# Transposing queries in float32 before the split, and a re-ordered opening, in an encoder kernel

## The chip, the cores and the metric

The kernel runs on one core of one Trainium2 chip. The metric is the device time of one execution in microseconds (us); the time before is the median of three runs. The engines are TensorE (PE, with its weight loads as PEld), VectorE (DVE), ScalarE (ACT), GpSimd (POOL) and SyncE (SP), which here only issues DMAs.

## The reference

Two layers of an encoder on x (256 tokens by 1024), float32. Each layer is a half-step feed-forward block, a mixing block with two attention branches, and a second half-step feed-forward block. Cut to what matters:

```
x = x + 0.5 * swiglu(rms_norm(x, ffn1_norm), ffn1_w_gate, ffn1_w_up, ffn1_w_down)
h = rms_norm(x, mix_norm);  z = h @ w_in
qa, ka, va, qs, ks, vs, zg = split(z)
qa, ka = rms_norm of each head (8 heads of 64);  qs (8 heads), ks (2 heads) likewise
o_na = neighbourhood_attention(qa, ka, va, na_rpb)      # 4 x 64 grid
o_sw = sliding_window_gqa(qs, ks, vs, t5_bias, sink)    # +-128 tokens
y = sigmoid(g_A) * (o_na @ w_branch_na) + sigmoid(g_B) * (o_sw @ w_branch_sw)
x = x + y @ w_out
x = x + 0.5 * swiglu(rms_norm(x, ffn2_norm), ...)       # 1024 -> 2816 -> 1024
```

## The kernel before

**Products in two parts.** Every float32 weight is loaded as `raw` (two rows of 128 by 512 at a time, ring of 4), then split into two fp32r tiles: `wh` is a copy made by ACT (L181), `wl` is the rest, made by DVE (L182); both lie in rings of 6. Activations are split the same way. A product is three 512-column matmuls (L167 to L169): hi by hi, hi by lo, lo by hi.

**Order.** PE's instructions run in the order in which the code emits them. What is not projected right away is put on a list by `defer` and emitted some ticks later, a tick being three matmuls of 512 columns; transpositions and attention fronts are laid between the matmuls of other projections in this way. A scheduler places the instructions of the other engines.

**Opening.** Layer 0's first feed-forward block begins with `opening`: the norm of x, the four weight pieces of column block c=0, then the squares for the row norms (ACT L214, DVE L218 and L219, POOL L173), and `second`, the four pieces of column block c=1. The gate of a column block is `sg` (ACT L448) and `hh` (DVE L449), once for each half t of the tokens. `hh` empties one of the two PSUM banks named `g`, and the projection after next writes that bank. `constants` loads the gains `qkg`, the mask and the sinks, and scales the gains on DVE (L106).

**Feed-forward.** Eleven column blocks c of 256 hidden units. The products of some of them with w_d use sums and differences of blocks; for three of these, `prepare` loads and forms the differences u and v of w_d's blocks (DVE L346) and splits them (uh, ul, vh, vl) while w_gu is still being projected: c=3 prepares 1, c=5 prepares 3, c=7 prepares 6.

**Queries.** In `mix`, a projection of 512 columns (8 heads of 64) for one half t of the tokens is normed per head (`normed`: z, sq, hv, rs_y, qn), split into `qs` with the hi and lo part of a head side by side, and 16 ticks later (18 for Q1) `turn` transposes it: one transposition for each head, 128 columns of fp32r, with hi in the first 64 partitions of the result and lo in the other 64. Two ACT copies (L499) reverse the query order and write `sqT` or `qT`. There are four such calls in a layer: Q0, Q1 (window attention) and q0, q1 (grid attention). The keys `kn` (`keys`: K0, K1, k0, k1) are transposed in float32 and split on the way out of PSUM by ACT L516 and DVE L517 into `skT` or `kT`. The first scores `sc` (L553) need Q0, Q1, K0 and K1. `qn` lies in a ring of two shared with `sq` and other tiles (tag xg), `qs` and `kn` in another ring of two (tag qk).

Of the kernel before, what the change touches and what calls it, by code (L numbers as in the profile page):

```python
# [11 lines left out]
F32 = mybir.dt.float32  # L12
F32R = mybir.dt.float32r
# [8 lines left out]
P = 128  # L22
# [28 lines left out]
HEAD = 128  # L51
PLAN = "SFGFGGFGGSS"
PREP = {3: 1, 5: 3, 7: 6}
NS = sum(kind != "S" for kind in PLAN)


@with_exitstack
def hybrid_encoder(ctx, tc, x, w_gu1, w_d1, w_in, b_gate, qk_gain, rpb, sink, t5,
# [27 lines left out]

    ident = const.tile([P, P], F32, name="ident")
    make_identity(nc, ident)
    ident_r = const.tile([P, P], F32R, name="ident_r")
    nc.vector.tensor_copy(ident_r, ident)  # L90
    mhalf = const.tile([P, 8], F32, name="mhalf")
    nc.vector.memset(mhalf, -0.5)
    warm = const.tile([P, 1], F32, name="warm")
# [6 lines left out]
    def constants():  # L100
        with tc.issue_after(rstd_done[0].ins):
            nc.gpsimd.dma_start(qkg, qk_gain)
            nc.gpsimd.dma_start(mask, c_mask)
            nc.gpsimd.dma_start(snk, bass.AP(tensor=sink.tensor, offset=sink.offset, ap=[[0, P], [1, L * NH]]))
        for g in (0, 2):
            nc.vector.scalar_tensor_tensor(qkg[:, :, g + 1], qkg[:, :, g + 1], 1.0 / math.sqrt(DH), qkg[:, :, g],  # L106
                                           op0=ALU.mult, op1=ALU.mult)
        nc.vector.tensor_scalar(nsnk, snk, -1.0, None, op0=ALU.mult)
# [113 lines left out]
    def opening(w, l):  # L222
        def piece(i, c=0):
            return load(w[l, 2 * i * P:(2 * i + 2) * P, c * 512:(c + 1) * 512].rearrange("(k p) n -> p k n", p=P),
                        2, 512)

        ps = [ps_g.tile([P, 512], F32, name="g", tag="g") for _ in range(T)]

        def steps(t, i):
            wh, wl = pieces[i]  # L230
            xh, xl = xT[t]
            for a, b in ((xh, wh), (xl, wh), (xh, wl)):
                for k in (2 * i, 2 * i + 1):
                    nc.tensor.matmul(ps[t], a[:, k, :], b[:, k % 2, :], start=a is xh and b is wh and k == 0,  # L234
                                     stop=b is wl and k == KD - 1)
            tick(2)

        pieces = []
        chain["act"] = warmed
        warmup(5)  # L240
        norm(0, 0, 0, True)
        pieces.append(piece(0))
        warmup(5)
        fetch(1, 0)
        norm(1, 0, 0, True)
        pieces.append(piece(1))
        fetch(0, 1)
        fetch(1, 1)
        warmup(3)
        steps(0, 0)  # L250
        norm(0, 0, 1, True)
        steps(1, 0)
        pieces.append(piece(2))
        norm(1, 0, 1, True)
        pieces.append(piece(3))
        square(0, 0, idle)
        square(0, 1, idle)
        second = [piece(0, 1)]
        square(1, 0, idle)
        square(1, 1, idle)  # L260
        second += [piece(i, 1) for i in range(1, KD // 2)]
        chain.clear()
        for i in (1, 2, 3):
            for t in range(T):
                steps(t, i)
        defer(24, "constants", constants)
        return ps, second

    def project(t, pieces, n):
# [34 lines left out]
    def ffn(l, n, w_gu, w_d, after):  # L304
        with tc.tile_pool(name="ffn", bufs=1) as fp:
# [128 lines left out]
            for c in range(NFC):  # L434
# [4 lines left out]
                    pieces = second  # L439
                else:  # L440
                    pieces = columns(w_gu, l, c * 512, 512)
                if c in PREP:
                    prepare(PREP[c])
                pair = act.tile([P, T, FC], F32, name="hh", tag="xg", bufs=2)
                for t in range(T):
                    ps = both[t] if first else project(t, pieces, 512)
# [25 lines left out]
    def mix(l, n, after):  # L472
        with tc.tile_pool(name="mix", bufs=1) as mp:
# [11 lines left out]
                                        r.unsqueeze(2).to_broadcast([P, nh, DH]), ALU.mult)  # L485

            def queries(key, ps, t, qT):
                qn = act.tile([P, NH, DH], F32, name="qn", tag="xg", bufs=2)
                normed(ps, t, NH, qn)
                qs = mp.tile([P, NH, 2, DH], F32R, name="qs", tag="qk", bufs=2)  # L490
                split_to(qs[:, :, 0, :], qs[:, :, 1, :], qn)

                def turn():
                    for half in range(2):
                        tp = ps_tp.tile([P, 4, P], F32R, name="tp", tag="tp")
                        for j in range(4):
                            nc.tensor.transpose(tp[:, j, :], qs[:, 4 * half + j].rearrange("p two d -> p (two d)"),
                                                ident_r)
                        nc.scalar.activation(qT[:, 4 * half:4 * half + 4, t * P:(t + 1) * P], flipped(tp), AF.Copy)  # L499

                defer(QK_LAG + MORE.get(key, 0), key, turn)

# [23 lines left out]
            def attend(name, ins, qT, kh, kl, kidx, bias_of, vcol, ready, oT, sink_l=None):  # L526
# [12 lines left out]
                def front(h):  # L539
# [10 lines left out]
                    sm = small.tile([P, T], F32, name="sm", tag="sm")  # L550
                    for t in range(T):
                        for i, k in enumerate((kh, kl)):
                            nc.tensor.matmul(ps[:, t, :], qT[:, h, t * P:(t + 1) * P], k[:, kidx(h), :],  # L553
                                             start=i == 0, stop=i == 1)
                    for t in range(T):
                        nc.vector.tensor_tensor_reduce(S_[:, t, :], ps[:, t, :], b(t), -1.0, least,  # L556
# [44 lines left out]
                both = mp.tile([P, 2, *shape], F32R, name=name, tag=tag)  # L601
                return both[:, 0], both[:, 1]

            sqT = mp.tile([P, NH, S], F32R, name="sqT", tag="sq")
            skT = pair("skT", "sk", [2, S])
            sv = mp.tile([P, T, 2, 3 * DH], F32R, name="sv")
            qT = mp.tile([P, NH, S], F32R, name="qT")
            kT = (mp.tile([P, NH, S], F32R, name="kh", tag="kh"), mp.tile([P, NH, S], F32R, name="kl"))
            va = mp.tile([P, T, NH, P], F32R, name="va")
            oB = pair("oB", "oB", [4, T, P])  # L610
# [219 lines left out]
```

## Time and profile before

| | before |
|---|---|
| median of 3 runs (1077.96 to 1079.82) | 1078.34 us |
| profiled execution, own time | 1079.11 us |
| its span, first to last instruction | 1077.3 us |
| PE busy | 1069.9 us, 99% |
| DVE busy | 876.0 us, 81% |
| ACT busy | 671.9 us, 62% |
| POOL busy | 116.5 us, 11% |
| granted TensorE clock, mean | 0.999 |

The own time lies 1.8 us over the span; that much passes around the instructions. PE is busy nearly all the time; the other engines are read here by where PE waits for them.

### The profile page before, as it was taken

What the parts mean: (1) busy time and instruction counts of PE and PEld (TensorE: products, weight loads), DVE (VectorE), ACT (ScalarE), POOL (GpSimd) and SP (SyncE); (2) the same over time, 40 slices, a digit from 0 to 9 for tenths busy, and PEclk for the clock granted to TensorE, in tenths of its full rate; (3) what the DMA queues carried; (4) which work ended last, traced back from release to release, by engine and by line L of the source; (5) the groups of instructions that cost most, each with busy time, mean ns of one, the idle gap of its engine ahead of it and who ended that gap; (6) DMA issues with size and microseconds to landing.
All of it is one profiled execution on the core that took longest, in us unless ns stands there. A gap on an engine that the chain in (4) does not pass through costs nothing.

```text
span 1077.3 us, 14747 instructions
## 1 busy us (share of the span) xinstructions
PE 1069.9 (99%) x5125; PEld 890.8 (83%) x5125; DVE 876.0 (81%) x1337; ACT 671.9 (62%) x1014; POOL 116.5 (11%) x118
## 2 busy tenths in 40 slices
PE   9999999999999999999999999999999999999998
PEld 7888888888888888888878888888888888888887
DVE  6788798889886768879877787988898866778796
ACT  6565654788764556565465665657887646566562
POOL 1000030243420000000000000003534100000000
PEclk9999999999999999999999999999999999999999
DMA  7777565765654567756647765548566554776652
GB/s 241 233 248 236 181 201 181 215 195 159 192 193 136 192 202 244 240 175 201 202 158 233 227 212 201 192 149 241 181 196 179 184 172 161 232 231 207 200 194 78
DMA packets 98827, 212.63 MB, mean 197 GB/s; under 512 B 7568, under 2 KB 13744, under 8 KB 98752
## 3 DMA queue, kind: packets, MB, share of 16 engines
q1 hardware_dynamic: 98560, 211.60, 62.2%
q8 instruction: 40, 0.66, 0.2%
q14 instruction: 35, 0.29, 0.1%
q0 software_dynamic: 192, 0.08, 0.1%
HBM read 210.59 MB, written 1.06 MB: 196 GB/s over the span
## 4 chain that ended last, share of the span: by engine, by line
PE 96%; DVE 2%; DMA 1%; issue 1%; ACT 0%; ACTq 0%; DVEq 0%
PE g L167 21%; PE g L169 21%; PE g L168 21%; PE acc L167 5%; PE acc L169 5%; PE acc L168 5%; PE tp L314 2%; PE sc L553 1%; PE po L588 1%; PE tp L169 1%; PE tp L167 1%; PE tp L168 1%; PE pt L574 1%; DMA raw<-in_w_gu 1%; PE tp L198 1%; PE g L234 1%
## 5 line engine op out<-in xcount | busy, mean ns | idle before, releaser
L182 DVE TENSOR_TENSOR wl<-raw,wh 128x1024 fp32r<-128x1024 f32 x336 | 404.9, 1217 | 71.8 <-ACT wh L181 69.7
L181 ACT ACTIVATE wh<-raw 128x1024 fp32r<-128x1024 f32 x336 | 346.5, 1044 | 132.4 <-DMA raw<-in_w_gu 50.2
L167 PE MATMUL g<-wh,xh 128*128 128x512 f32 (+1 forms) x976 | 383.9, 393 | 0.5 <-DVE hh L449 0.5
L168 PE MATMUL g<-wl,xh 128*128 128x512 f32 (+1 forms) x976 | 377.6, 387 | 1.1 <-DVE wl L182 1.1
L169 PE MATMUL g<-wh,xl 128*128 128x512 f32 (+1 forms) x976 | 377.9, 387 | 0.7 <-DVE xl L182 0.7
L169 PEld LDWEIGHTS g<-wh,xl 128*128 128x128 f32 x976 | 183.3, 188 | 40.0 <-DVE xl L182 2.1
L168 PEld LDWEIGHTS g<-wl,xh 128*128 128x128 f32 x976 | 183.7, 188 | 34.6 <-DVE wl L182 1.9
L167 PEld LDWEIGHTS g<-wh,xh 128*128 128x128 f32 x976 | 183.6, 188 | 33.8 <-DVE hh L449 1.1
L448 ACT ACTIVATE sg<-g,rs_y 128x256 f32<-128x256 f32 x88 | 41.1, 467 | 85.8 <-PE g L169 73.6
L449 DVE SCALAR_TENSOR_TENSOR hh<-g,rs_y,sg 128x256 f32<-128x256 f32 x88 | 42.2, 479 | 49.6 <-ACT sg L448 49.5
L167 PE MATMUL acc<-wh,hi 128*128 128x512 f32 x180 | 71.1, 395 | 0.0
L169 PE MATMUL acc<-wh,lo 128*128 128x512 f32 x180 | 70.2, 390 | 0.0
L168 PE MATMUL acc<-wl,hi 128*128 128x512 f32 x180 | 70.1, 389 | 0.0
L173 POOL TENSOR_TENSOR rs_y<-ms,mhalf 128x1 f32<-128x1 f32 x12 | 6.7, 557 | 554.8 <-DVE ms L219 546.4
L346 DVE TENSOR_TENSOR u<-raw 128x512 f32<-128x512 f32 x64 | 41.9, 685 | 18.2 <-DMA raw<-in_w_d 18.1
L181 ACT ACTIVATE corner<-raw 128x512 fp32r<-128x512 f32 x32 | 20.2, 631 | 50.6 <-DMA raw<-in_w_d 28.3
L566 POOL TENSOR_TENSOR S<-S,sm 128x512 f32<-128x512 f32 x32 | 37.2, 1161 | 65.6 <-DVE sm L565 42.4
L169 PEld LDWEIGHTS acc<-wh,lo 128*128 128x128 f32 x180 | 33.8, 188 | 7.2
L168 PEld LDWEIGHTS acc<-wl,hi 128*128 128x128 f32 x180 | 33.8, 188 | 6.8
L167 PEld LDWEIGHTS acc<-wh,hi 128*128 128x128 f32 x180 | 33.8, 188 | 6.7
L559 ACT ACTIVATE S<-S,mx 128x256 f32<-128x256 f32 x64 | 31.9, 499 | 8.0 <-DVE mx L556 7.9
L182 DVE TENSOR_TENSOR lo<-a,hi 128x896 fp32r<-128x896 f32 x32 | 33.7, 1083 | 0.0
(189 smaller groups left out, 1511.7 us busy)
## 6 DMA issues: line engine op xcount, KB each, us to landing
raw<-in_w_gu SPq DMA_DIRECT2D x176, 512.0 KB, 4.4
raw<-in_w_d SPq DMA_DIRECT2D x100, 512.0 KB, 4.1
raw<-in_w_in SPq DMA_DIRECT2D x64, 512.0 KB, 4.5
raw<-in_w_out SPq DMA_DIRECT2D x16, 512.0 KB, 3.6
bb<-in_b_gate SPq DMA_DIRECT2D x16, 256.0 KB, 3.7
raw<-in_w_bsw SPq DMA_DIRECT2D x8, 512.0 KB, 3.8
raw<-in_w_bna SPq DMA_DIRECT2D x8, 512.0 KB, 3.6
raw<-in_w_d SPq DMA_DIRECT2D x12, 256.0 KB, 2.5
```

What stands on the lines that cost most here:

```text
L167: nc.tensor.matmul(ps, xh, wh, start=first, stop=False)
L168: nc.tensor.matmul(ps, xh, wl, start=False, stop=False)
L169: nc.tensor.matmul(ps, xl, wh, start=False, stop=last)
L181: linked("act", lambda: nc.scalar.activation(hi, src, AF.Copy))
L182: linked("dve", lambda: nc.vector.tensor_tensor(lo, src, hi.bitcast(F32), ALU.subtract))
L198: nc.tensor.transpose(tp[:, i, :], xs[t][:, k * P:(k + 1) * P], ident)
L314: nc.tensor.transpose(tp[:, SLOT[t][i], :], hh[:, t, i * P:(i + 1) * P], ident)
L346: sub = lambda to, x, y: nc.vector.tensor_tensor(to, x, y, ALU.subtract)
L448: nc.scalar.activation(sg, ps[:, :FC], AF.Silu, scale=rstd[t])
L449: nc.vector.scalar_tensor_tensor(pair[:, t], ps[:, FC:], rstd[t], sg, op0=ALU.mult, op1=ALU.mult)
L559: nc.scalar.activation(S_[:, t, :], S_[:, t, :], AF.Exp, bias=mx[:, t:t + 1], scale=-1.0, accum_out=sm[:, t:t + 1])
L566: nc.gpsimd.tensor_tensor(S_, S_, sm.unsqueeze(2).to_broadcast([P, T, S]), ALU.mult)
```

## The change

Four things change. (1) `queries` no longer splits before it transposes. `qn` takes the place of `qs` in the ring qk, four float32 transpositions turn two heads each, and the split is done from PSUM: for even and for odd heads one ACT copy and one DVE subtraction of 64 partitions by 4 heads by 128. In `sqT` and `qT` the even heads now stand ahead of the odd ones, and the score matmul indexes them so; hi and lo of a head still fill 128 partitions. `ident_r` and its cast are gone. (2) In the opening, two pieces of c=1 instead of one stand ahead of the squares of x1. (3) The scaling of `qkg` and `snk` is emitted at tick 70 and no longer with their loads. (4) In the first feed-forward block alone, the three `prepare` calls stand at c=5, 7 and 8.

```
-PREP = {3: 1, 5: 3, 7: 6}
+PREP = {3: 1, 5: 3, 7: 6}
+PREP_FIRST = {5: 1, 7: 3, 8: 6}
...
-    ident_r = const.tile([P, P], F32R, name="ident_r")
-    nc.vector.tensor_copy(ident_r, ident)
...
+    def scaled():
         for g in (0, 2):
             nc.vector.scalar_tensor_tensor(qkg[:, :, g + 1], ...)
...
-        second = [piece(0, 1)]
+        second = [piece(i, 1) for i in range(2)]
         square(1, 0, idle)
         square(1, 1, idle)
-        second += [piece(i, 1) for i in range(1, KD // 2)]
+        second += [piece(i, 1) for i in range(2, KD // 2)]
...
         defer(24, "constants", constants)
+        defer(70, "scaled", scaled)
...
-                if c in PREP:
-                    prepare(PREP[c])
+                prep = PREP if n else PREP_FIRST
+                if c in prep:
+                    prepare(prep[c])
...
             def queries(key, ps, t, qT):
-                qn = act.tile([P, NH, DH], F32, name="qn", tag="xg", bufs=2)
+                qn = mp.tile([P, 2, NH, DH], F32, name="qn", tag="qk", bufs=2)[:, 0]
                 normed(ps, t, NH, qn)
-                qs = mp.tile([P, NH, 2, DH], F32R, name="qs", tag="qk", bufs=2)
-                split_to(qs[:, :, 0, :], qs[:, :, 1, :], qn)
 
                 def turn():
-                    for half in range(2):
-                        tp = ps_tp.tile([P, 4, P], F32R, name="tp", tag="tp")
-                        for j in range(4):
-                            nc.tensor.transpose(tp[:, j, :], qs[:, 4 * half + j].rearrange("p two d -> p (two d)"),
-                                                ident_r)
-                        nc.scalar.activation(qT[:, 4 * half:4 * half + 4, t * P:(t + 1) * P], flipped(tp), AF.Copy)
+                    tp = ps_tp.tile([P, 4, P], F32, name="tp", tag="tp")
+                    for j in range(4):
+                        nc.tensor.transpose(tp[:, j, :], qn[:, 2 * j:2 * j + 2].rearrange("p two d -> p (two d)"), ident)
+                    cols = slice(t * P, (t + 1) * P)
+                    for e in range(2):
+                        a, b = e * DH, (1 - e) * DH
+                        split_to(qT[a:a + DH, e, :, cols], qT[b:b + DH, e, :, cols], flipped(tp[a:a + DH]))
...
-                            nc.tensor.matmul(ps[:, t, :], qT[:, h, t * P:(t + 1) * P], k[:, kidx(h), :],
+                            nc.tensor.matmul(ps[:, t, :], qT[:, h % 2, h // 2, t * P:(t + 1) * P], k[:, kidx(h), :],
```

The changed file is one to three lines longer, so L181 and L182 become L182 and L183, L448 and L449 become L451 and L452, and so on.

DVE in the opening, before: `wl_219`, `wl_232`, `wl_238` and `wl_244` are the four pieces of c=1, `hh_283` the gate of c=0 (`g_107` the bank of its first half).

```order
L182 TENSOR_TENSOR wl_219<-raw_216,wh_218 128x1024
L449 SCALAR_TENSOR_TENSOR hh_283<-g_107,rs_y_214,sg_284 128x256
L218 TENSOR_TENSOR ms_224<-ssq_140 128x1
L219 TENSOR_SCALAR ms_224<-ms_224 128x1
L182 TENSOR_TENSOR wl_232<-raw_229,wh_231 128x1024
L182 TENSOR_TENSOR wl_238<-raw_235,wh_237 128x1024
L106 SCALAR_TENSOR_TENSOR qkg_94<-qkg_94 128x2 x2
L182 TENSOR_TENSOR wl_244<-raw_241,wh_243 128x1024
L449 SCALAR_TENSOR_TENSOR hh_283<-g_108,rs_y_227,sg_287 128x256
```

The same place on DVE with the change; the four pieces are `wl_217`, `wl_223`, `wl_236` and `wl_242`.

```order
L183 TENSOR_TENSOR wl_217<-raw_214,wh_216 128x1024
L183 TENSOR_TENSOR wl_223<-raw_220,wh_222 128x1024
L452 SCALAR_TENSOR_TENSOR hh_281<-g_105,rs_y_212,sg_282 128x256
L219 TENSOR_TENSOR ms_228<-ssq_138 128x1
L220 TENSOR_SCALAR ms_228<-ms_228 128x1
L183 TENSOR_TENSOR wl_236<-raw_233,wh_235 128x1024
L183 TENSOR_TENSOR wl_242<-raw_239,wh_241 128x1024
L452 SCALAR_TENSOR_TENSOR hh_281<-g_106,rs_y_231,sg_285 128x256
L107 SCALAR_TENSOR_TENSOR qkg_92<-qkg_92 128x2 x2
```

The second piece now stands ahead of the first gate, and the scaling of the gains stands behind the second gate instead of between two pieces. On ACT the copy of the second piece moves in the same way, ahead of the first square of x1, with `sg` of the first half behind that square as before.

DVE in the window between the transposition of Q1 and the first scores of layer 0, before: `skT` are the two halves of the window attention's keys, `kn_2042` the normed K1, `qn_2106` and `qs_2117` belong to q1.

```order
L481 TENSOR_REDUCE hv_2111<-sq_2109 128x8
L484 TENSOR_TENSOR kn_2042<-z_2043,rs_y_2050 128x2x64
L482 TENSOR_SCALAR hv_2111<-hv_2111 128x8
L182 TENSOR_TENSOR wl_2200<-raw_2197,wh_2199 128x1024
L182 TENSOR_TENSOR wl_2206<-raw_2203,wh_2205 128x1024
L484 TENSOR_TENSOR qn_2106<-z_2107,rs_y_2114 128x512
L517 SCALAR_TENSOR_TENSOR skT_1813<-tp_2145,qkg_94,skT_1813 128x2x128
L182 TENSOR_TENSOR wl_2357<-raw_2354,wh_2356 128x1024
L182 TENSOR_TENSOR wl_2363<-raw_2360,wh_2362 128x1024
L517 SCALAR_TENSOR_TENSOR skT_1813<-tp_2162,qkg_94,skT_1813 128x2x128
L182 TENSOR_TENSOR qs_2117<-qn_2106,qs_2117 128x8x64
```

The same place with the change; `tp_2113` is Q1's transposed block, and the two rows that read it write the low parts of its even and odd heads.

```order
L487 TENSOR_TENSOR kn_2031<-z_2032,rs_y_2039 128x2x64
L484 TENSOR_REDUCE hv_2100<-sq_2098 128x8
L485 TENSOR_SCALAR hv_2100<-hv_2100 128x8
L183 TENSOR_TENSOR wl_2180<-raw_2177,wh_2179 128x1024
L183 TENSOR_TENSOR sqT_1810<-tp_2113,sqT_1810 64x4x128
L183 TENSOR_TENSOR wl_2186<-raw_2183,wh_2185 128x1024
L519 SCALAR_TENSOR_TENSOR skT_1811<-tp_2128,qkg_92,skT_1811 128x2x128
L487 TENSOR_TENSOR qn_2095<-z_2096,rs_y_2103 128x512
L183 TENSOR_TENSOR wl_2331<-raw_2328,wh_2330 128x1024
L183 TENSOR_TENSOR sqT_1810<-tp_2113,sqT_1810 64x4x128
L183 TENSOR_TENSOR wl_2337<-raw_2334,wh_2336 128x1024
L519 SCALAR_TENSOR_TENSOR skT_1811<-tp_2145,qkg_92,skT_1811 128x2x128
```

Two subtractions now stand between `kn` and the second `skT`; the split of q1 that followed the second `skT` is gone from there.

DVE in column block c=3 of the first feed-forward block, before: the pieces of w_gu are the rows `wl`, and `u_486`, `ul1_490` belong to `prepare`.

```order
L346 TENSOR_TENSOR u_486<-raw_484,raw_482 128x512
L346 TENSOR_TENSOR u_486<-raw_482 128x512
L182 TENSOR_TENSOR lo4_408<-tp_397,hi4_407 128x512
L327 TENSOR_TENSOR a_413<-a_413 128x128 x3
L182 TENSOR_TENSOR wl_473<-raw_470,wh_472 128x1024
L327 TENSOR_TENSOR a_413<-a_413 128x128
L182 TENSOR_TENSOR ul1_490<-u_486,uh1_489 128x1024
L182 TENSOR_TENSOR wl_479<-raw_476,wh_478 128x1024
L182 TENSOR_TENSOR lo7_412<-a_413,hi7_411 128x896
L182 TENSOR_TENSOR wl_560<-raw_557,wh_559 128x1024
L449 SCALAR_TENSOR_TENSOR hh_371<-g_430,rs_y_227,sg_455 128x256
```

The same place with the change, where the rows of `prepare` are missing.

```order
L183 TENSOR_TENSOR lo4_406<-tp_395,hi4_405 128x512
L329 TENSOR_TENSOR a_411<-a_411 128x128 x4
L183 TENSOR_TENSOR wl_468<-raw_465,wh_467 128x1024
L183 TENSOR_TENSOR lo7_410<-a_411,hi7_409 128x896
L183 TENSOR_TENSOR wl_474<-raw_471,wh_473 128x1024
L183 TENSOR_TENSOR wl_537<-raw_534,wh_536 128x1024
L452 SCALAR_TENSOR_TENSOR hh_369<-g_425,rs_y_231,sg_450 128x256
```

The three u and ul rows ahead of the last `hh` are gone, and with them their loads of w_d on SP's queue; PE's order is as before but for the eight blocks of transpositions.

## Rows read from the trace of the kernel before

**Rows 1.** The page: span, PE's busy line, the chain by engine.

```profile
span 1077.3 us, 14747 instructions
...
PE 1069.9 (99%) x5125; PEld 890.8 (83%) x5125; DVE 876.0 (81%) x1337; ACT 671.9 (62%) x1014; POOL 116.5 (11%) x118
...
PE 96%; DVE 2%; DMA 1%; issue 1%; ACT 0%; ACTq 0%; DVEq 0%
```

**Rows 2.** The waits of PE: total us, times, longest.

```profile
PE g L168 <- DVE wl L182: 1.1, 2, 0.7
...
PE g L167 <- DVE hh L449: 0.5, 1, 0.5
```

**Rows 3.** The timeline of PE in the opening: start, us, engine, line.

```profile
20.28 0.45 PE L167 MATMUL g<-wh,xh 128*128 128x512 f32 x1
20.57 0.40 PE L168 MATMUL g<-wl,xh 128*128 128x512 f32 x1
20.80 0.40 PE L169 MATMUL g<-wh,xl 128*128 128x512 f32 x1
...
27.48 0.40 PE L167 MATMUL g<-wh,xh 128*128 128x512 f32 x1
```

**Rows 4.** The timeline of ACT in the opening.

```profile
17.33 1.04 ACT L181 ACTIVATE wh<-raw 128x1024 fp32r<-128x1024 f32 x1
18.28 0.58 ACT L214 ACTIVATE idle<-x 128x512 f32<-128x512 f32 x1
...
19.18 0.47 ACT L448 ACTIVATE sg<-g,rs_y 128x256 f32<-128x256 f32 x1 [0.20 <-PE g L234]
```

**Rows 5.** The timeline of DVE in the opening.

```profile
18.41 1.23 DVE L182 TENSOR_TENSOR wl<-raw,wh 128x1024 fp32r<-128x1024 f32 x1 [0.60 <-ACT wh L181]
19.69 0.48 DVE L449 SCALAR_TENSOR_TENSOR hh<-g,rs_y,sg 128x256 f32<-128x256 f32 x1
```

**Rows 6.** The timeline of PE at the end of column block c=3.

```profile
49.91 0.39 PE L169 MATMUL g<-wh,xl 128*128 128x512 f32 x1
50.78 0.50 PE L167 MATMUL g<-wh,xh 128*128 128x512 f32 x1 [0.48 <-DVE hh L449]
51.12 0.39 PE L168 MATMUL g<-wl,xh 128*128 128x512 f32 x1
```

**Rows 7.** The timeline of DVE in column block c=3.

```profile
42.09 1.29 DVE L346 TENSOR_TENSOR u<-raw 128x512 f32<-128x512 f32 x2 [2.53 <-DMA raw<-in_w_d]
```

**Rows 8.** The timeline of PE: a float32 block of the norm, then Q1's block.

```profile
185.67 0.60 PE L198 MATMUL tp<-ident,x 128*128 128x128 f32 x4
186.03 0.48 PE L167 MATMUL acc<-wh,hi 128*128 128x512 f32 x1
...
217.28 0.80 PE L497 MATMUL tp<-ident_r,qs 128*128 128x128 f32 x8
217.92 0.46 PE L167 MATMUL g<-wh,xh 128*128 128x512 f32 x1
```

**Rows 9.** Groups of DVE by line and shape: busy us, mean ns.

```profile
L182 DVE TENSOR_TENSOR pl<-pt,ph 128x512 fp32r<-128x512 f32 x32 | 21.8, 680 | 2.8 <-ACT ph L181 2.7
...
L182 DVE TENSOR_TENSOR qs<-qn,qs 128x512 fp32r<-128x512 f32 x8 | 5.5, 682 | 0.0
```

**Rows 10.** The timeline of DVE between Q1's block and the first scores.

```profile
217.50 0.69 DVE L481 TENSOR_REDUCE hv<-sq 128x8 f32<-128x512 f32 x1 [1.02 <-ACT sq L479]
218.19 0.29 DVE L484 TENSOR_TENSOR kn<-z,rs_y 128x128 f32<-128x128 f32 x1
...
225.38 0.48 DVE L517 SCALAR_TENSOR_TENSOR skT<-tp,qkg,skT 128x256 fp32r<-128x256 f32 x1
```

**Rows 11.** The timeline of PE at the first scores.

```profile
226.03 0.64 PE L553 MATMUL sc<-skT,sqT 128*128 128x256 f32 x4
```

**Rows 12.** Windows of the first feed-forward block: busy us and instructions of each engine.

```profile
95.40:107.10 11.70, 11.70 (x53) 9.63 (x52) 9.91 (x11) 6.98 (x8) 0.00 (x0) 1.00 0.90 290
107.10:118.90 11.80, 11.80 (x58) 9.85 (x57) 9.30 (x16) 7.47 (x10) 0.00 (x0) 1.00 0.58 187
```

More of the change, by code (lines that the diff above doesn't have):

```diff
@@ L602, in pair @@
                 return both[:, 0], both[:, 1]
-            sqT = mp.tile([P, NH, S], F32R, name="sqT", tag="sq")
+            sqT = mp.tile([P, 2, NH // 2, S], F32R, name="sqT", tag="sq")
             skT = pair("skT", "sk", [2, S])
             sv = mp.tile([P, T, 2, 3 * DH], F32R, name="sv")
-            qT = mp.tile([P, NH, S], F32R, name="qT")
+            qT = mp.tile([P, 2, NH // 2, S], F32R, name="qT")
             kT = (mp.tile([P, NH, S], F32R, name="kh", tag="kh"), mp.tile([P, NH, S], F32R, name="kl"))
```

## The prediction

> **What bounds the kernel now.** I read the page first: PE is busy 1069.9 of 1077.3 us and holds 96% of the chain that ended last [rows 1]. Time therefore goes only by PE's own instructions, or by the few moments in which PE waits. The view of PE's waits is short: two waits on `wl` (1.1 us together) and one on `hh` (0.5 us) concern this change [rows 2]; the two on `wl` stand in column block c=1, the one on `hh` at the end of c=3. Then I read PE's starts in the timelines, because they price a wait or a block of transpositions better than the modelled durations do: a 512-column matmul follows the one before after 0.23 us (20.57 to 20.80) [rows 3]. DVE is the engine that PE waits for, so its order decides what the edits beside it cost.
>
> **Queries: what PE saves.** A block of eight fp32r transpositions holds the next matmul back by 217.92 - 217.28 = 0.64 us; a block of four float32 transpositions holds it back by 186.03 - 185.67 = 0.36 us [rows 8]. The new block is of the second kind, float32, 128 by 128, four of them, so PE saves 0.28 us a call, 0.56 for the two calls of a branch, and 2.24 us for eight calls, if nothing takes it back. Two heads side by side are to PE one more float32 tile of 128 by 128, as those of `x` are; I see no row from which the new ones could cost more.
>
> The Trainium skill, "FP8 and Floating Point Precision", section "TensorE Precision Notes", says that true FP32 takes four passes through the PE array, which speaks against this edit. By that rule, with a quarter of eight fp32r transpositions' 0.64 us (0.08 us) as one pass, four float32 ones would take 4 x 4 x 0.08 = 1.28 us instead of 0.36, and each call would lose 0.64 us. The rows of four float32 transpositions show 0.36 us, so the rule as it stands doesn't hold for these blocks, and the measurement decides.
>
> **Queries: what the other engines do.** Before, a call costs DVE one subtraction from SBUF (`qs`, 0.682 us); now it costs two of 64 partitions by 512 elements from PSUM. The nearest row is `pl` from `pt`, 0.680 us for 512 elements in each of 128 partitions [rows 9]. I take 0.68 each, since the elements in a partition are as many; an end below would be half of that, if partitions counted. DVE is thus 0.68 us a call longer; ACT has one copy less. More important is where they stand: before, the split came long before the transposition, now it lies behind it.
>
> The first scores of the window attention start at 226.03 on PE [rows 11], and the last DVE instruction that they need is the second `skT`, 225.38 + 0.48 = 225.86 [rows 10]. There is 0.17 us of slack. PE would like to be there 0.56 us sooner, at 225.47. I replay DVE from `kn` of K1. It waits for a buffer of the ring qk which Q1's block gives back, so it starts no sooner than the end of that block, about 0.5 us sooner than the 218.19 of before, say 217.65. With the change these follow back to back by the order shown: kn 0.21, hv 0.61, its scaling 0.17, wl 1.15, sqT 0.6, wl 1.15, skT 0.45, qn 0.6, wl 1.15, sqT 0.6, wl 1.15, skT 0.48 (from start to start, for which I take 0.08 us off each duration; wl by the 1.23 of [rows 5]). The sum is 8.3 us, end at about 226.0. Subtractions of 64 partitions that are cheaper by up to 0.25 us each would bring the end to 225.5. So the first scores would start between 225.6 and 226.2, and of the 0.56 us of Q0 and Q1 between 0.4 and -0.2 us is kept; I take 0.1. PE waits there in exchange for what it saved.
>
> For q0 and q1 nothing waits so closely: the pieces between them and the grid attention are many, so their 0.56 us are kept; the lower end is 0, if DVE, which is full through the fronts of the window attention, makes a later transposition wait. A layer gives 0.1 + 0.56 = 0.66, both layers 1.32 us; the ends are -0.4 and 2.24.
>
> **Opening.** Before, c=1 starts at 20.28 as soon as the first `hh` has left the bank (19.69 + 0.48 = 20.17) [rows 3, 5], and its second half starts at 27.48: 7.20 us for 24 matmuls. Without waits these take 0.29 + 23 x 0.231 = 5.60 us, so the two waits on `wl` and the slow restarts behind them cost 1.60 us. With the change ACT makes the copy of the second piece from 18.28 for 0.95 us, then the square of x1 (0.70 with the read of its sum), then `sg` at 19.93 instead of 19.18, for 0.47 us [rows 4]. DVE does the first `wl` from 18.41, the second from 19.55 to 20.77, then `hh` to 21.16. c=1 therefore starts at 21.27, 0.99 us later: a new wait, on `hh`. By then the second piece lies ready, the third follows at 23.2 (needed at 24.3) and the fourth at 24.4 (needed at 25.7), so no wait is left in it (after `sg` ACT makes the second square of x1 to 21.1 and the copies to 22.05 and 23.0, DVE's subtractions follow them; the pieces' first `wl` matmuls are the 14th and the 20th), and the second half starts at 21.27 + 5.60 = 26.87. The opening gains 0.61 us. At worst it gains nothing (the third piece late by as much); at best, if `sg` is placed as soon as before, 1.3. Scaling `qkg` behind the second gate costs nothing: DVE waits there for the gains' load, now with no urgent piece behind it, and the first reader is the keys' turn some 200 us on. The 0.16 us cast of `ident_r` lay before PE had work.
>
> **Prepare at c=5, 7 and 8.** At c=3 PE goes from 49.91 to 50.78 for one matmul, and 0.34 to the next, in place of 2 x 0.23: 0.75 us [rows 6]. It waits for an `hh` that stands on DVE behind two `u` (1.29 us [rows 7]) and one `ul` (1.2, as any `wl`). With these 2.5 us gone `hh` is no longer last, and the 0.75 us are gained. What is late next is nothing that I found.
>
> The other side is c=8. A prepare is 2 x 1.29 for u and v and 2 x 1.2 for the splits, 5.0 us of DVE, with two loads of w_d on SP's queue ahead of those of c=9. DVE is idle for 1.79 + 2.50 = 4.29 us in the two windows in which it would fall [rows 12]. The 0.7 us that do not fit shift into the window behind, where DVE has more room. I cost it at nothing; the bounds are 0 and the whole 5.0 us, if the instructions of `prepare` stand in front of a piece that PE is waiting for.
>
> **Sum.** 0.61 + 0.75 + 1.32 = 2.68 us. Against the profiled execution's own time, 1079.11, this gives 1076.43. That execution lies 0.77 us over the median of the runs shown, 1078.34, and the runs differ by up to 1.86 us; the result is a median too, so I forecast 1078.34 - 2.68 = 1075.7 us.
>
> **The rivals.** (a) All of it is kept: the subtractions of 64 partitions are short, or the scheduler's order leaves `skT` ahead of need. The gain is 0.61 + 0.75 + 2.24 = 3.6, 1074.7 us. For it speaks that DVE stands idle in the seconds before K1; against it the 0.17 us of slack at the scores.
> (b) The mix gives nothing: DVE's two extra subtractions delay `skT` and then the chain of the window attention's fronts in both layers as much as PE saved. The gain is 1.36, 1077.0 us. For it speaks that DVE is the engine waited for; against it that q0 and q1 are transposed where PE's next need is far.
> (c) The opening gives nothing, since the later `hh` starts a chain of late pieces: 2.07 us of gain, 1076.3.
> (d) On the other side: `prepare` at c=8 stands on PE's path whole. From the point at which its u and v stand ahead of the pieces of c=9 or of the last gates, each us of it is one of PE's; slower than before needs 2.68 us of the 5.0, and all of it gives 1078.34 - 2.68 + 5.0 = 1080.7 us. For it speaks that 5.0 are more than the 4.29 idle; against it that the window behind has room.
> (e) The float32 transpositions cost four passes (the rule of the page above): each call loses 0.64, 5.1 us in all, and with the opening's and c=3's gains it is 1078.34 - 1.36 + 5.1 = 1082.1 us. The rows of float32 blocks speak against it.
>
> **How the numbers follow.** The forecast has 0.50, (a) 0.17, (b) 0.20, (c) 0.05, (d) 0.07, (e) 0.01. The range goes from (a) to (b), which with (c) leave out 0.08, each widened by half of the runs' spread, 0.93 us: 1073.8 to 1077.9 us. What 0.2% is here, 2.16 us, is about what a measurement of this kernel can tell from no change; it stands at 1076.2, half a us above the forecast. Faster by more: four fifths of the forecast, nearly all of (a), a little of (b) and (c), 0.60. Slower by more: (d) and (e), with half of (d) only partly paid, 0.05. The rest, 0.35, is within 0.2%.
>
> **What the profile after would show.** Right: the new blocks hold PE for 0.36 us; PE's waits on `wl` in c=1 are gone and one on `hh` stands at about 21.3; c=1's second half starts near 26.9; no wait near 50; a short wait of the first scores on `skT` in each layer (0.3 to 0.5 us); DVE busy up by 8 x 0.68 = 5.4 us. Wrong: waits on `wl` or `hh` between 95 and 141; waits of the window attention's transpositions on DVE or ACT; a block of queries that holds PE for longer than 0.36 us; or a time above 1077.9 us, which would mean that a load or a late piece in the moved `prepare` has reached PE.

## The result, and the profile after

The changed kernel takes 1081.53 us (median of 12 runs, 1080.92 to 1083.49) against 1078.59 us for the kernel before (12 runs): a ratio of 1.0028, with a 95% interval of 1.0020 to 1.0036. It is slower by 2.9 us, where 2.7 us of gain were forecast. The profiled execution has a span of 1079.8 us and 1081.58 us of its own.

The page says at once where to look, in the busy line and the chain by engine, which answer to [rows 1].

```profile
span 1079.8 us, 14671 instructions
...
PE 1069.2 (99%) x5093; PEld 887.8 (82%) x5093; DVE 883.1 (82%) x1344; ACT 667.7 (62%) x1006; POOL 120.8 (11%) x118
...
PE 89%; DVE 6%; issue 2%; ACT 2%; DMA 1%; POOL 0%; POOLq 0%; DVEq 0%; ACTq 0%
```

PE has less to do, and still the span is longer. In the chain PE's share fell from 96 to 89%, and DVE's rose from 2 to 6%. DVE is busy for 7.1 us more: the subtractions add the 5.4 us expected, and the rest lies in other instructions, some of which took longer and some shorter than before. The view of PE's waits, in total us, times and longest, answers to [rows 2]:

```profile
PE tp L516 <- DVE qT L183: 1.2, 2, 0.6
PE pt L576 <- POOL S L568: 1.1, 2, 0.7
PE tp L516 <- DVE skT L519: 1.0, 2, 0.5
PE g L168 <- DVE hh L452: 0.8, 1, 0.8
PE g L170 <- DVE xl L183: 0.7, 1, 0.7
PE sc L555 <- DVE skT L519: 0.3, 2, 0.2
PE tp L168 <- DVE lo L183: 0.2, 1, 0.2
```

The waits on `wl` and the one at the end of c=3 are gone. In their place stand four in the mix block, each twice, once a layer: the second half of the key block k0 waits for the split of q0, the scores' transposition waits for POOL's S, the key block K1 waits for `skT`, and so do the first scores.

PE runs the same matmuls in the same order in both kernels but for the query blocks, so the start of each can be set against its partner. The table gives how far PE is behind the kernel before (negative: ahead), in us, at five places, named by the time in the kernel before. It is worked out from start times in both traces, and it serves for the experiments too.

| kernel | 51 (c=3 done) | 209 (before Q0) | 260 (after k1) | 741 (layer 1's mix) | end |
|---|---|---|---|---|---|
| changed | -1.29 | -0.84 | 0.94 | 1.00 | 2.49 |
| open_only | -1.33 | -0.61 | -0.62 | -0.59 | -0.52 |
| query_only | -1.16 | -0.56 | 1.19 | 2.03 | 4.16 |
| hi_first | -1.39 | -1.28 | 0.37 | 0.28 | 1.88 |
| no_sub | -1.42 | -1.06 | -2.13 | -1.84 | -2.94 |
| dummy_load | -1.45 | -1.08 | 1.15 | 1.09 | 3.33 |
| new_Q | -1.43 | -1.50 | -1.39 | -1.29 | -1.21 |
| new_q | -1.45 | -1.23 | 0.03 | 0.25 | 2.04 |
| new_Q_chain | -1.46 | -0.28 | 0.36 | 0.56 | 1.19 |

Up to 51 us the changed kernel gains 1.29 us against this execution of the kernel before, as forecast (1.36). But `query_only`, which has the old opening and the old `prepare`, is 1.16 us ahead there too. The two executions of the old opening differ in the load of the gains: DVE waits for it ahead of the fourth piece of c=1 in the kernel before (the first of these lines) and not in `query_only` (the second).

```profile
24.79 0.23 DVE L106 SCALAR_TENSOR_TENSOR qkg<-qkg 128x2 f32<-128x2 f32 x2 [1.19 <-DMA qkg<-in_qk_gain]
23.68 0.23 DVE L104 SCALAR_TENSOR_TENSOR qkg<-qkg 128x2 f32<-128x2 f32 x2
```

The load took 3.5 us from issue to landing in the one and 2.4 in the other, and 4.0 to 5.3 us in the kernels with the new opening. So what the opening gains hangs on when this load lands, and one execution of the kernel before doesn't show what it gains as a rule.

Between 51 and 209 us most kernels that are ahead give back some of their lead, nearly all at 146 us, among the first products with w_d (0.43 us in the changed kernel, 1.03 in `new_Q_chain`). Then each mix block costs 1.5 to 1.8 us net, where it was to gain 0.66.

How this comes about shows in the timeline of the changed kernel, the rows of the query split and of K1's block (start, us, engine, line):

```profile
216.18 0.60 PE L497 MATMUL tp<-ident,qn 128*128 128x128 f32 x4
216.53 0.48 PE L168 MATMUL g<-wh,xh 128*128 128x512 f32 x1
...
217.40 0.57 ACT L182 ACTIVATE sqT<-tp 64x512 fp32r<-64x512 f32 x1
...
219.14 0.69 DVE L183 TENSOR_TENSOR sqT<-tp,sqT 64x512 fp32r<-64x512 f32 x1
...
220.89 0.59 ACT L182 ACTIVATE sqT<-tp 64x512 fp32r<-64x512 f32 x1
...
221.63 0.41 PE L516 MATMUL tp<-ident,kn 128*128 128x128 f32 x2 [0.51 <-DVE skT L519]
...
223.25 0.69 DVE L183 TENSOR_TENSOR sqT<-tp,sqT 64x512 fp32r<-64x512 f32 x1
```

The block itself holds PE for 216.53 - 216.18 = 0.35 us. But copy, subtraction, copy and subtraction of Q1 run strictly one behind the other, and the PSUM bank stays taken until 223.94, 7.8 us. There are two such banks: K1's block waits until `skT` of K0 has been read out of the other one. The other wait, on S, goes with a full DVE; these are the windows around it, with busy us of PE, PEld, DVE, ACT and POOL. First the kernel before:

```profile
235.00:245.00 10.00, 10.00 (x61) 8.60 (x60) 8.60 (x18) 8.49 (x22) 5.71 (x5) 1.00 0.75 243
245.00:255.00 10.00, 10.00 (x60) 8.61 (x59) 9.94 (x24) 9.41 (x21) 3.79 (x4) 1.00 0.62 163
```

Then the changed kernel:

```profile
235.00:245.00 10.00, 9.41 (x55) 7.93 (x54) 9.88 (x23) 8.36 (x21) 5.08 (x5) 1.00 0.80 247
245.00:255.00 10.00, 9.64 (x55) 7.94 (x53) 9.94 (x20) 8.16 (x20) 4.92 (x5) 1.00 0.51 135
```

DVE had 1.4 us to spare in the first window and 0.06 in the second. With the change it is full for 20 us.

### The profile page after: what moved, and what is told of

It reads as the page before. It is cut to its first block, busy times and chain, and to the rows that moved or that the text cites. A ratio compares the mean times of both kernels' runs of the same rounds, so it can differ in the third digit from the quotient of the medians.

```text
span 1079.8 us, 14671 instructions
## 1 busy us (share of the span) xinstructions
PE 1069.2 (99%) x5093; PEld 887.8 (82%) x5093; DVE 883.1 (82%) x1344; ACT 667.7 (62%) x1006; POOL 120.8 (11%) x118
## 3 DMA queue, kind: packets, MB, share of 16 engines
HBM read 210.59 MB, written 1.06 MB: 196 GB/s over the span
## 4 chain that ended last, share of the span: by engine, by line
PE 89%; DVE 6%; issue 2%; ACT 2%; DMA 1%; POOL 0%; POOLq 0%; DVEq 0%; ACTq 0%
PE g L170 20%; PE g L168 20%; PE g L169 20%; PE acc L168 5%; PE acc L170 5%; PE acc L169 5%; DVE wl L183 2%; PE tp L316 2%; PE tp L168 1%; PE tp L169 1%; PE tp L170 1%; PE po L590 1%; PE sc L555 1%; PE pt L576 1%; PE tp L199 1%
## 5 line engine op out<-in xcount | busy, mean ns | idle before, releaser
L183 DVE TENSOR_TENSOR wl<-raw,wh 128x1024 fp32r<-128x1024 f32 x336 | 402.9, 1212 | 70.1 <-ACT wh L182 67.7
L182 ACT ACTIVATE wh<-raw 128x1024 fp32r<-128x1024 f32 x336 | 346.8, 1045 | 134.3 <-DMA raw<-in_w_gu 50.0
L451 ACT ACTIVATE sg<-g,rs_y 128x256 f32<-128x256 f32 x88 | 41.1, 467 | 86.8 <-PE g L170 74.7
L452 DVE SCALAR_TENSOR_TENSOR hh<-g,rs_y,sg 128x256 f32<-128x256 f32 x88 | 42.1, 479 | 50.0 <-ACT sg L451 50.0
L182 ACT ACTIVATE corner<-raw 128x512 fp32r<-128x512 f32 x32 | 20.2, 633 | 51.1 <-DMA raw<-in_w_d 30.7
L568 POOL TENSOR_TENSOR S<-S,sm 128x512 f32<-128x512 f32 x32 | 39.7, 1241 | 61.0 <-DVE sm L567 31.0
L183 DVE TENSOR_TENSOR lo<-a,hi 128x896 fp32r<-128x896 f32 x32 | 33.8, 1084 | 0.6 <-ACT hi L182 0.6
```

The costliest lines, as they stand in the source:

```text
L182: linked("act", lambda: nc.scalar.activation(hi, src, AF.Copy))
L183: linked("dve", lambda: nc.vector.tensor_tensor(lo, src, hi.bitcast(F32), ALU.subtract))
L451: nc.scalar.activation(sg, ps[:, :FC], AF.Silu, scale=rstd[t])
L452: nc.vector.scalar_tensor_tensor(pair[:, t], ps[:, FC:], rstd[t], sg, op0=ALU.mult, op1=ALU.mult)
L568: nc.gpsimd.tensor_tensor(S_, S_, sm.unsqueeze(2).to_broadcast([P, T, S]), ALU.mult)
```

## The experiments

The kernel before ran beside each group of experiments, at medians of 1078.8 to 1079.1 us; the ratios are to those runs.

**The parts apart.** `open_only` has the queries of before and all the rest of the change; `query_only` is the kernel before with the new `queries` alone.

> The changed kernel with the queries of before (split, then eight fp32r transpositions a call), so only the opening, the later prepare calls and the later scaling are left. By the trace of the changed kernel PE was 1.18 us ahead after column block c=3 and lost 0.34 us of it near 146 us. If these parts are independent of the queries, this kernel gains 0.85 us: about 1077.7 us against 1078.6. If the later prepare calls are what made the change slow, it is slower than before.

Measured: 1078.54 us, ratio 0.9998 (0.9989 to 1.0007). 0.85 us of gain cannot be told from none by this interval; the trace of it is 0.52 us ahead at the end. The opening is not the loss.

> The kernel before with the new queries alone. If the loss lies in the queries, PE saves 8 x 0.28 = 2.2 us and loses some 5 us in waits in the two mix blocks, as in the changed kernel: about 3.7 us slower than before, 1082.3 us. If the opening is to blame, it is no slower than before.

Measured: 1082.93 us, ratio 1.0036 (1.0023 to 1.0048). The loss is the queries', about 4 us of it.

**Chain or load.** In `hi_first` both copies stand ahead of both subtractions:

```
+                    for e in range(2):
+                        nc.scalar.activation(hi[e], src[e], AF.Copy)
+                    for e in range(2):
+                        nc.vector.tensor_tensor(qT[b:b + DH, e, :, cols], src[e], hi[e].bitcast(F32), ALU.subtract)
```

> The changed kernel, with both ACT copies of a query block emitted ahead of both DVE subtractions; the work is the same. Chain theory: copy, subtraction, copy, subtraction run strictly one behind the other, the second copy waits for the first subtraction, and the PSUM bank of the block stays taken some 7 us, so that the key blocks wait for a bank. Then the waits of the key transpositions (2.2 us idle) go, the fronts of the window attention are in time again, and the kernel lands at 1076 to 1077 us. Load theory: the 0.68 us that DVE has more in each call is the cost, wherever it stands; then this kernel stays within 0.5 us of the changed one, at 1081 to 1082 us.

Measured: 1081.19 us, ratio 1.0024 (1.0014 to 1.0033). The time is that of the load theory, yet the chain theory was right about the waits; these are PE's waits there:

```profile
PE pt L580 <- POOL S L572: 3.0, 4, 1.1
...
PE sc L559 <- DVE skT L523: 0.6, 2, 0.3
```

No key block waits for a bank any more, and the wait on S has grown from 1.1 to 3.0 us. The two limits stand one behind the other: what PE no longer waits for a bank, it waits for the fronts. The timeline of DVE there shows them:

```profile
239.64 1.39 DVE L505 TENSOR_TENSOR qT<-tp,qT 64x512 fp32r<-64x512 f32 x2
...
241.06 0.69 DVE L484 TENSOR_REDUCE hv<-sq 128x8 f32<-128x512 f32 x1
```

The subtractions of q0 stand ahead of `hv`, `pl`, `kl` and the next S without a gap.

`no_sub` leaves the subtractions out (two whole ACT copies fill the halves, so the low parts of the queries are copies of a high part); it bounds what is to be had.

```
-                        split_to(qT[a:a + DH, e, :, cols], qT[b:b + DH, e, :, cols], flipped(tp[a:a + DH]))
+                        nc.scalar.activation(qT[:, e, :, cols], flipped(tp), AF.Copy)
```

> The changed kernel without the subtractions: two ACT copies of 128 partitions fill the halves, so the low parts of the queries hold copies of a high part. DVE is then lighter than before by 0.68 us a call and the bank waits for ACT alone. Both theories: PE keeps all of 8 x 0.28 = 2.2 us beside the 0.85 of the opening, about 1075.5 us. If it stays above 1078, the float32 transpositions or the ring that the normed queries moved to cost something by themselves.

Measured: 1076.29 us, ratio 0.9977 (0.9968 to 0.9987). All eight blocks keep 0.28 us each, and no wait is left in the mix blocks. The float32 transpositions and the move to the ring qk cost nothing.

`dummy_load` keeps the old queries and adds one DVE instruction a call that nobody needs:

```
+                    nc.vector.tensor_tensor(junk, done_q, done_q, ALU.add)
```

> The queries of before, with one extra DVE instruction a call (128 x 512, adding a finished copy of four transposed heads to itself, result unused) behind the transpositions; the rest as in the changed kernel. DVE load is that of the changed kernel, and no PSUM bank is held longer. Load theory: about 0.68 us of DVE work at a full DVE delays the fronts of the window attention, so against the kernel with the old queries (1078.5 us) this one loses 2 to 4 us, 1080.5 to 1082.5 us, with waits of the score transpositions on POOL's S. Bank theory: it stays within 0.7 us of 1078.5 us.

Measured: 1082.69 us, ratio 1.0034 (1.0022 to 1.0047), with 2.8 us of waits on S in four places. So no bank need be held for the loss. But the added instruction's result also takes a place in the ring xg: `sq` of k0 starts at 231.83 on ACT, right behind the split of q0 (231.01 + 0.69 = 231.70), where in the kernel before it started at 230.31. This run alone doesn't part the DVE work from that delay; `new_q` below has no such tile.

**Which calls.** `new_Q` has the new form (copies first) in Q0 and Q1 alone, `new_q` in q0 and q1 alone; `queries_old` is the function of before.

```
+                "q": lambda t: queries_old(f"q{t}", unit(0, 512, t), t, qT),
```

The line is of `new_Q`; `new_q` has it for "Q".

> The new form (both ACT copies first) for Q0 and Q1 alone, the old form for q0 and q1. With new queries in all four calls and the copies first, the waits of the window attention's score transpositions cost 2 us in a layer and the first scores 0.5. Load theory: those waits come from the subtractions of q0 and q1, which stand among the fronts on DVE, so here only the 0.5 us at the first scores is lost against 0.56 saved: 1078 to 1079 us.

Measured: 1078.67 us, ratio 0.9999 (0.9990 to 1.0008).

> The new form (both ACT copies first) for q0 and q1 alone, the old form for Q0 and Q1. Load theory: the waits of the window attention's score transpositions stay, 1.5 to 2 us in a layer against 0.56 saved: 1080.5 to 1082 us. If the waits came from Q0 and Q1, this one is at 1077.5 us.

Measured: 1081.10 us, ratio 1.0020 (1.0012 to 1.0029), with the 3.0 us of waits on S. So the DVE work that costs is that of q0 and q1, which falls among the window attention's fronts. At Q0 and Q1 it costs what it saves: 0.6 us of waits on `skT` at the first scores in both layers.

`new_Q_chain` is `new_Q` with copies and subtractions alternating as in the change.

> New queries for Q0 and Q1 alone, with copy, subtraction, copy, subtraction one behind the other as in the changed kernel; q0 and q1 in the old form. It differs from the kernel with the copies first (1078.7 us) by the order of four instructions a call. Bank theory for this place: the key block K1 waits for a PSUM bank as in the changed kernel (0.66 us a layer with its restart), and the time is 1.0 to 1.3 us above that of the kernel with the copies first, 1079.7 to 1080.0 us. If the place is bound by DVE's amount of work whichever way the copies stand, the two are equal within 0.5 us.

Measured: 1079.79 us, ratio 1.0006 (0.9997 to 1.0015), 1.1 us above `new_Q`. Its waits have K1's two back (1.0 us in all). Where nothing takes their place, the alternating order costs what its waits show.

**Other ways to split.** `one_sub` makes one subtraction of 128 partitions and puts the low parts in place by two more ACT copies; `one_sub_nocopy` leaves these two copies out (the low parts are then unused).

```
+                    nc.vector.tensor_tensor(low, flipped(tp), qT[:, 0, :, cols].bitcast(F32), ALU.subtract)
+                    for e in range(2):
+                        a, b = e * DH, (1 - e) * DH
+                        nc.scalar.activation(qT[b:b + DH, e, :, cols], low[a:a + DH], AF.Copy)
```

> The changed kernel with one DVE subtraction of 128 partitions a call instead of two of 64: two ACT copies of the whole block, one subtraction of the block, two ACT copies of 64 partitions that put the low parts in their halves. DVE has as much to do as before the change, ACT 1.2 us a call more than in the changed kernel. Load theory: the late fronts go, and most of what the kernel without subtractions reached (1076.3 us) is kept: 1076 to 1077.5 us. If it is the place behind the transposition and not the amount that counts, it stays near 1079.5 us or above.

Measured: 1081.09 us, ratio 1.0020 (1.0011 to 1.0029). My expectation failed: DVE does as much as before the change, and PE waits in other places.

```profile
PE sc L559 <- DVE skT L523: 1.8, 2, 0.9
PE g L168 <- DVE va L530: 1.8, 2, 1.1
```

> The kernel with one subtraction a call, without the two ACT copies that put the low parts in their halves (the low parts of the queries are then never used, and their halves hold copies of a high part). It differs from the kernel without subtractions (1076.3 us) by one DVE subtraction a call behind the transposition. If the extra ACT copies made the kernel with one subtraction slow (1081.1), this one is at 1076.3 to 1077.5 us. If one subtraction at that place on DVE is enough to make the fronts late, it is at 1079 to 1081 us.

Measured: 1076.99 us, ratio 0.9983 (0.9974 to 0.9991). One subtraction a call behind the transposition is harmless; it was the two ACT copies a call that made `one_sub` slow. In `one_sub` ACT is busy for 9.88 of 10 us from 215 to 225, ahead of the wait on `skT` (8.28 in the kernel before), and for 9.45 us from 245 to 255, ahead of the one on `va` (9.41 before).

`late_q` copies q0 and q1 whole into SBUF and holds their subtractions back behind a later front; `pool_q` gives them to POOL, with Q1's and K1's blocks earlier.

```
+                        nc.scalar.activation(qx, tp, AF.Copy)
+                        defer(LATE, key, lambda: divide(cols, qx))
...
+                                order.enter_context(tc.issue_after(front_done[0].ins))
...
+                        engine = nc.vector if key[0] == "Q" else nc.gpsimd
```

The first three lines are of `late_q`, the last one of `pool_q`.

> New queries in all four calls. Q0 and Q1 as with the copies first; q0 and q1 are copied whole by ACT out of PSUM into SBUF and split there 24 ticks later, the subtractions held back on DVE until a later front of the window attention is done. DVE does as much as in the changed kernel, ACT one copy of 0.59 us more for q0 and q1. Place theory: it is not the 0.68 us a call that costs, but that it stands among the first fronts while DVE is full (9.94 of 10 us from 245 to 255); then the waits of the score transpositions go, and 0.56 us of PE time a layer is kept: 1077 to 1078 us. Amount theory: DVE then makes a later front late by as much, 1079.5 to 1081 us.

Measured: 1084.52 us, ratio 1.0057 (1.0043 to 1.0071), the slowest. The waits on S are gone, and PE waits 4.8 us on `va` (which empties a `g` bank) and 1.4 us on `o`. The place theory fails as I put it: this later place, with one more ACT copy, was worse. A better place was not tried.

> New queries in all four calls, with the earlier blocks of Q1 and K1; for q0 and q1 ACT copies the block whole into SBUF, and GpSimd (POOL) makes the two subtractions in place of DVE. DVE then has 0.68 us a call less to do for q0 and q1 than in the kernel before, POOL some 2 us a call more, ahead of or between the products S, which the fronts need too. If a full DVE alone is the bound, the fronts are in time and 0.56 us a layer more is kept than with the old form of q0 and q1 (1077.9 us): 1076.7 to 1077.5 us. If POOL's S, or ACT's third copy, comes late instead, it is at 1079 us or more.

Measured: 1082.83 us, ratio 1.0035 (1.0021 to 1.0049). POOL takes 1.431 us on the mean for a subtraction of 64 x 512 and makes it ahead of S; PE waits 4.3 us on S in two places (in the profiled execution, at 1084.69 us the slowest of the five).

**A faster version.** `new_Q_early` is `new_Q` with Q1's block two ticks and K1's one tick earlier. `early_prep_same` has, besides, the old `PREP` in all blocks.

```
-MORE = {"Q1": 2, ("sw", 4): 1.5, ("na", 4): 2, ("na", 5): 1.5}
+MORE = {"Q1": 0, "K1": -1, ("sw", 4): 1.5, ("na", 4): 2, ("na", 5): 1.5}
...
-                prep = PREP if n else PREP_FIRST
+                prep = PREP
```

> The kernel with the new form for Q0 and Q1 alone (1078.7 us), with Q1's block two ticks and K1's block one tick earlier on PE (1.4 and 0.7 us). There the first scores wait 0.3 us for the second half of skT in each layer. If that wait is DVE's subtractions ahead of skT, an earlier start of the chain takes it away: 0.5 us a layer less, about 1077.7 us. If DVE is full there anyhow, or the key block then waits for a bank, no change: 1078.7 us or more.

Measured: 1077.87 us, ratio 0.9991 (0.9982 to 1.0000). The waits on `skT` are gone.

> The fastest kernel so far (new form for Q0 and Q1, earlier blocks, 1077.9 us) with the prepare calls of the first feed-forward block back at c=3, 5 and 7. If moving them is worth what the trace says, the wait on hh at the end of c=3 comes back, 0.75 us with its restart; as the products near 146 us wait for a load in nearly all kernels that are ahead there, up to 0.5 us of it is not seen in the end: 1078.1 to 1078.6 us. If the opening's two parts give nothing in the end, it is at 1077.9.

Measured: 1077.84 us, ratio 0.9989 (0.9980 to 0.9998). It is ahead of both kernels, of the kernel before by 0.1%, which the interval barely parts from none. The wait at c=3 did not come back with the `prepare` calls, against the expectation. This is DVE there:

```profile
40.80 1.30 DVE L350 TENSOR_TENSOR u<-raw 128x512 f32<-128x512 f32 x2 [1.88 <-DMA raw<-in_w_d]
...
48.96 0.47 DVE L454 SCALAR_TENSOR_TENSOR hh<-g,rs_y,sg 128x256 f32<-128x256 f32 x1
```

The same u waits for the same load, but ends the wait 1.3 us sooner than at 42.09 in [rows 7], and `hh` follows at 48.96 instead of 50.26, ahead of PE. That the opening gives its `raw` buffers back sooner, and the loads so start sooner, fits this; it was not tried apart.

## Why the prediction was wrong

**The step that failed** is the cost of the queries' DVE work, "For q0 and q1 nothing waits so closely". I asked when PE next needs q0 and q1, and found that time far off. The lower end of that step does name a full DVE and a late transposition, but lets them take no more than the 0.56 us saved in a layer, and no row gave that bound. The extra 0.68 us a call was right in size (0.688 to 0.689 us on the mean for each subtraction); its price at q0 and q1 was put at 0 and is 1.82 us in the first layer and 2.35 in the second: `new_q` falls back by 1.26 us in the first mix block (-1.23 to 0.03) and by 1.79 in the second (0.25 to 2.04), although its two blocks save 0.56 in each. That the second DVE subtraction of q0 and q1 is the cause is shown by `new_Q` against `new_q`, and, for all four calls together, by `hi_first` (1081.19 us) against `one_sub_nocopy` (1076.99 us), which has one subtraction a call less and as many ACT copies.

**How it costs so much.** The right question was what the subtractions stand in front of on DVE: the window attention's fronts. These rows of the kernel before are its third and fourth front, with POOL's S and PE's transposition `pt`:

```profile
246.16 1.03 POOL L566 TENSOR_TENSOR S<-S,sm 128x512 f32<-128x512 f32 x1
247.98 1.21 DVE L182 TENSOR_TENSOR wl<-raw,wh 128x1024 fp32r<-128x1024 f32 x1
248.14 0.60 PE L574 MATMUL pt<-ident,S 128*128 128x128 f32 x4
249.11 0.15 DVE L564 TENSOR_TENSOR sm<-sm,es 128x2 f32<-128x2 f32 x1
249.66 0.16 DVE L565 RECIPROCAL sm<-sm 128x2 f32<-128x2 f32 x1
249.99 1.04 POOL L566 TENSOR_TENSOR S<-S,sm 128x512 f32<-128x512 f32 x1 [2.24 <-PE g L169]
254.53 0.60 PE L574 MATMUL pt<-ident,S 128*128 128x128 f32 x4
```

The fourth front in the changed kernel:

```profile
249.06 2.37 DVE L183 TENSOR_TENSOR wl<-raw,wh 128x1024 fp32r<-128x1024 f32 x2
250.37 0.28 ACT L565 ACTIVATE es<-mx,snk 128x2 f32<-128x2 f32 x1
252.16 0.15 DVE L566 TENSOR_TENSOR sm<-sm,es 128x2 f32<-128x2 f32 x1
252.83 1.21 DVE L183 TENSOR_TENSOR wl<-raw,wh 128x1024 fp32r<-128x1024 f32 x1
253.97 0.15 DVE L567 RECIPROCAL sm<-sm 128x2 f32<-128x2 f32 x1
254.29 1.04 POOL L568 TENSOR_TENSOR S<-S,sm 128x512 f32<-128x512 f32 x1 [5.08 <-ACT va L525]
255.38 0.66 PE L576 MATMUL pt<-ident,S 128*128 128x128 f32 x4 [0.75 <-POOL S L568]
```

At the third front S ended 0.95 us ahead of PE (246.16 + 1.03 = 247.19, against 248.14); `new_q` loses 0.41 us there in the first layer and 0.42 in the second. At the fourth front S ended 3.5 us ahead, and yet `new_q` loses more there, 1.23 us in each layer. More than the added work stands in the way: DVE's order is another. In the kernel before `sm` follows one `wl`, and the reciprocal comes 0.55 us after it. In the changed kernel two `wl` and the next front's first two instructions stand ahead of `sm`, though `es` was ready at 250.65, and `pl` and a third `wl` stand ahead of the reciprocal. This order stands in the changed kernel, `query_only`, `hi_first`, `new_q` and `dummy_load`, in both layers, and in no other run. As these rows read, the price goes at least in part by the place that the scheduler gave to other work. No run has the added work in the old order; how much of the price is the work itself and how much the order stays open.

**A second miss** is the order inside a call. I read that the split moves behind the transposition, but not that the second copy waits for the first subtraction, so the bank is held for 7.8 us. `new_Q_chain` puts this at 1.1 us for Q0 and Q1. In the changed kernel it hardly adds to the time, since the fronts are late anyhow (`hi_first`: 0.3 us).

**The rivals.** (b) came nearest in mechanism: DVE's subtractions delay `skT` and then the fronts. Its price, "as much as PE saved", had no reason for an upper end; the waits come to more. Two of the prediction's signs of being wrong came, a transposition of the window attention (K1's) that waits on DVE and a time above 1077.9 us; but the time was to mean a late load or piece in the moved `prepare`, and that is not what happened. (d), prepare at c=8, did not occur: no wait stands between 95 and 141 us. Nor did (e): the block holds PE for 0.35 us, so the four passes of the Trainium skill ("FP8 and Floating Point Precision", "TensorE Precision Notes") don't show in this form of transposition. (The 0.08 us of the prediction's sum for it is an eighth of 0.64 us, one transposition, and not a quarter.)

**Right by its steps.** Each block saves 0.28 us. The first scores wait on `skT`, though for 0.16 us in each layer, where 0.3 to 0.5 were forecast; K1 just ahead of them waits for 0.51. In the opening c=1 starts at 21.38 (21.27 forecast), after a wait of 0.77 us on `hh`:

```profile
20.85 0.48 DVE L452 SCALAR_TENSOR_TENSOR hh<-g,rs_y,sg 128x256 f32<-128x256 f32 x1
```

and its second half starts at 26.95 (26.87 forecast).

**Right for a wrong reason.** The wait at c=3 went, but moving `prepare` was not needed for that: `early_prep_same` has no such wait either.

**Mis-sized.** Of the 1.3 us by which the opening is ahead of this execution of the kernel before only part reaches the end (0.52 us in the trace of `open_only`), and by the old opening of `query_only` most of it is a matter of when the gains land, which the prediction did not weigh. PE waits for a split again near 146 us; the forecast took a lead, once won, as kept. That those splits follow loads which don't come sooner is read from the order in the trace, and was not tried.

## What to carry to other kernels

Price an added instruction by what stands behind it on its own engine, not by when its result is needed: two extra times 0.68 us in a layer, with results that nobody waits for, cost PE some 2 us, since a chain that PE waits for stood behind them on a full engine. Read the engine's whole order again after such a change: here the scheduler also moved other work ahead of that chain, where 3.5 us of margin had been. An engine that is 81% busy on the mean can be 99% busy in the stage that matters; read the windows of that stage before giving it work, and those of the engine that is to take the work over too.
When a split moves to the far side of a transposition, its engines hold the PSUM bank: emit all copies out of the bank ahead of the subtractions, and count who needs the bank next.

## What the runs showed that was not expected

A DVE subtraction of 64 partitions by 512 takes 0.689 us, as one of 128 partitions does (0.680 [rows 9]). Halving the partitions saves nothing, and the two halves cost twice.

A DVE instruction beside POOL's work can be far slower. This is the norm of k1 in the changed kernel:

```profile
244.94 1.67 DVE L487 TENSOR_TENSOR kn<-z,rs_y 128x512 f32<-128x512 f32 x1
```

The fastest of the eight `qn`, of the same line and shape, takes 0.679 us, and here POOL's `b` ran from 244.87 for 1.20 us. The Trainium skill, "SBUF — State Buffer", section "SBUF: two separate sides", says that of a DVE instruction with two SBUF inputs and a GpSimd instruction that reads SBUF the one that starts first holds their shared port for the whole instruction, and the other waits. The rows agree roughly: `kn` starts 0.07 us behind `b`, which ends at 246.07, and a wait until then with 0.68 us of work would take 1.81 us, against 1.67 measured. No run here took POOL's work away to test it.
